# GLA score products of at most 32 rows, two low levels to a bank, and the decay of k to its tile's end on ScalarE alone

## The chip, the cores and the metric

The kernel runs on one core of a Trainium2 chip. Its time is the device time of one launch in microseconds (us). Before the change three runs took 2829.29, 2830.95 and 2833.31 us, so the median is 2830.95. One more execution was recorded by the hardware profiler.

The engines are called as in the profile: PE is TensorE (matrix products; PEld its weight loads), DVE is VectorE, ACT is ScalarE, POOL is GpSimd, SP is SyncE, which issues most DMAs. Each engine has one queue of instructions and takes them in order. PE writes only to PSUM, eight banks of 512 fp32 numbers on each of 128 partitions.

## The reference: what is computed

A streaming encoder of two layers, one with a retention mixer and one with gated linear attention (GLA), each followed by a convolutional feed-forward block, over 1024 frames of a new stream and 32 frames of a running one. The change touches the GLA mixer alone, whose core is, for each of 4 heads (q and k of 128, v of 256):

```python
def gla_chunk(S, xs):
    q, k, v, lg = xs
    b = jnp.cumsum(lg, axis=1)
    expo = b[:, :, None] - b[:, None, :]
    expo = jnp.where(causal[None, :, :, None, None], expo, -jnp.inf)
    A = jnp.einsum('bihd,bjhd,bijhd->bhij', q, k, jnp.exp(expo))
    intra = jnp.einsum('bhij,bjhe->bihe', A, v)
    cross = jnp.einsum('bihd,bhde->bihe', q * jnp.exp(b), S)
    bL = b[:, -1]
    S_new = jnp.exp(bL)[..., None] * S + jnp.einsum('bjhd,bjhe->bhde', k * jnp.exp(bL[:, None] - b), v)
    return S_new, intra + cross
```

The scores A weigh each pair of frames by a decay that differs by channel, exp(b_i - b_j). The factor k * exp(bL - b) carries k to the end of its tile for the state.

## The kernel before

**Units and tiles.** The 1056 frames are three spans (`CM`: 384, 384 and 288 frames). A unit is one head with one span; the 12 units go head by head. A span is cut into tiles of 128 frames (`minors`): three in the first two spans; in the third two, and one of the 32 frames of the running stream.

**Scores in levels.** Within a tile the pairs (j, i) are split by the block size s at which j and i part: for each s in 64, 32, 16, 8, 4, 2, 1, j lies in the first half of a block of 2s and i in the second. `weigh` makes for each level a tensor X[s] in which the first halves hold k times exp(b at the middle minus b) and the second halves q times exp(b minus b at the middle); one product of the two is the score. GpSimd subtracts (L968, L972), ScalarE takes the exponential (`expln`, L1189), VectorE multiplies (L970, L974). `weigh` also makes kd, which is k times exp(bL - b): GpSimd subtracts b at the tile's end (L988, three times a unit), ScalarE takes the exponential over the span, VectorE multiplies by k (L992), and ScalarE makes eL, exp(bL), tile by tile.

**The score products** (`scores`) are in fp32 and go into two PSUM banks, `lv0` and `lv1`, that `small()` hands out in turn. The first bank is zeroed by a product with a tile of zeros (L1001), and then gets for each tile the products of 32 frames with themselves (L1005) and the levels 64, 32 and 16 (L1010: products of 64, 32 and 16 rows). VectorE multiplies it by a mask into A (L1015). Each of the levels 8, 4, 2 and 1 has a bank of its own with products of 32 rows and 16 columns (L1023), from which VectorE copies the wanted elements into A under a mask (L1028). Then kd is transposed into the next bank (L1036), and A and kd are split in two parts of less precision each (L1044 to L1048, `stack_left` at L253 and L255).

**The rest of a unit.** `project` makes q, k and the gate of the next unit (L127 to L129, L936) in a pair of banks `pj`. `mix` makes v (`value`, L240 to L248), and per tile the state and the output (`attend`, L1117 to L1143). The last `attend` of a unit, its norm (`finish`, L1157 to L1164, which scales oraw) and its `store` come within the next unit: `store` transposes the output oraw in two halves (L1170) into the next two banks of `small()`, from which ScalarE copies (L1172) and a DMA stores.

**What sets the order.** The program is written in the order project (next unit), finish (last unit), scores, store (last unit), mix, weigh (next unit). When the kernel is built, a scheduler orders each engine's instructions by its own estimates and by the tiles' buffers: so value products stand between the score products, and the norm's small operations between the masks. At run time each engine keeps that order and waits by semaphores.

## Time and profile before

| | |
|---|---|
| median of 3 runs | 2830.95 us (2829.29 to 2833.31) |
| profiled execution | 2831.14 us, its span 2829.4 us, granted TensorE clock 0.997 |
| busy share of the span | PE 98%, PEld 94%, DVE 74%, ACT 47%, POOL 10% |
| GLA stage | about 1623 to 1943 us of the span: 320 us, the 12 units |
| in the GLA stage | PE busy 310 us, DVE 239, ACT 181, POOL 93 |

In the profile, a line number is that of the kernel before. A group row gives line, engine, operation, tiles as out<-in without buffer numbers, the shape and the count; then busy time and the mean time of one in ns; then the idle time of the engine ahead of it and what ended it. A timeline row gives the start and the length in us; for a group of several (x8) from the first start to the last end. A product's length holds its way through the array, so that products overlap: what one costs is read from start to start. Every fp32 score product has two records.

### The profile page before, as it was taken

To read this page: it belongs to the slowest core of one execution; us is meant where nothing else is said; L and a number is where in the kernel's file an instruction comes from. 1 tells how busy PE (TensorE), PEld (TensorE's weight loads), DVE (VectorE), ACT (ScalarE), POOL (GpSimd) and SP (SyncE) were. 2 spreads that over 40 slices of the span, in tenths; PEclk is the share of its full clock that TensorE was granted. 3 is DMA by queue.
4 is the path that set the end of the run, shared out by engine and by line. 5 is a ranking of instruction groups with operands and counts; after the bars stand their busy time and mean duration, and the time that the engine had idled before them with its cause. 6 is when DMAs were issued, how large, how long until landed. Compare 5 with 4: busy or idle time off the path is not lost.

```text
span 2829.4 us, 54448 instructions
## 1 busy us (share of the span) xinstructions
PE 2763.6 (98%) x21926; PEld 2654.8 (94%) x21926; DVE 2099.9 (74%) x3497; ACT 1318.5 (47%) x2384; POOL 285.6 (10%) x517
## 2 busy tenths in 40 slices
PE   8999999999999999999999999999999999999998
PEld 8999978888899999999999989989999999999997
DVE  7777777777587878887874687874378778878756
ACT  8433344444455544444543555553244444445434
POOL 1000000000001111111000133320020111110001
PEclk9999999999999999999999999999999999999999
DMA  6333386664866222432867401114522233428673
GB/s 222 108 123 106 110 281 205 212 201 153 273 196 203 66 86 99 149 117 87 285 204 234 159 30 52 52 45 156 187 87 74 81 109 122 145 76 278 204 236 113
DMA packets 232477, 419.47 MB, mean 148 GB/s; under 512 B 27392, under 2 KB 145792, under 8 KB 231200
## 3 DMA queue, kind: packets, MB, share of 16 engines
q1 hardware_dynamic: 231680, 415.40, 44.7%
q8 instruction: 171, 2.80, 0.4%
q14 instruction: 82, 0.67, 0.1%
q10 hardware_dynamic: 544, 0.59, 0.1%
HBM read 292.08 MB, written 123.85 MB: 147 GB/s over the span
## 4 chain that ended last, share of the span: by engine, by line
PE 82%; DVE 8%; DMA 5%; ACT 3%; issue 1%; POOL 1%; SPq 0%; DVEq 0%; ACTq 0%; POOLq 0%
PE pu L341 16%; PE pu L336 16%; PE pu L340 16%; PE pd L1316 3%; PE pd L1317 3%; PE pd L1318 3%; PE psv L242 2%; PE psv L241 2%; PE psv L240 2%; PE pj L127 1%; PE pj L128 1%; PE pj L129 1%; PE pg L127 1%; PE pg L128 1%; PE pg L129 1%
## 5 line engine op out<-in xcount | busy, mean ns | idle before, releaser
L106 DVE TENSOR_TENSOR wlo<-raw,whi 128x1024 fp32r<-128x1024 f32 (+1 forms) x147 | 180.7, 1235 | 91.8 <-ACT whi L106 38.0
L1572 ACT COPY AR<-pu 128x264 f32<-128x264 f32 x264 | 99.0, 375 | 293.9 <-PE pu L341 291.2
L341 PE MATMUL pu<-XA,wgl 128*128 128x264 f32 x752 | 213.6, 284 | 0.0
L336 PE MATMUL pu<-XA,wgh 128*128 128x264 f32 x752 | 213.0, 283 | 0.0
L340 PE MATMUL pu<-XA,wgh 128*128 128x264 f32 x752 | 213.0, 283 | 0.0
L106 ACT CAST whi<-raw 128x1024 fp32r<-128x1024 f32 (+1 forms) x147 | 152.6, 1041 | 109.9 <-DMA raw<-w_ro 37.5
L1316 PE MATMUL pd<-XB,whi 128*128 128x264 f32 x552 | 158.5, 287 | 1.7 <-DVE rm L212 1.7
L1594 DVE SCALAR_TENSOR_TENSOR AR<-AR,cw 128x1058 f32<-128x1058 f32 x88 | 116.0, 1318 | 58.1 <-ACT AR L1593 55.7
L1318 PE MATMUL pd<-XB,wlo 128*128 128x264 f32 x552 | 157.5, 285 | 0.0
L1317 PE MATMUL pd<-XB,whi 128*128 128x264 f32 x552 | 157.4, 285 | 0.0
L336 PE MATMUL pu<-XA,wsh 128*128 128x264 f32 x520 | 148.3, 285 | 1.7 <-ACT AR L1572 0.9
L341 PE MATMUL pu<-XA,wsl 128*128 128x264 f32 x520 | 147.9, 284 | 0.8 <-DVE wsl L309 0.8
L309 DVE TENSOR_TENSOR wtl<-rv,wth 128x1024 fp32r<-128x1024 f32 x58 | 71.5, 1234 | 102.0 <-ACT wth L309 96.3
L340 PE MATMUL pu<-XA,wsh 128*128 128x264 f32 x520 | 147.3, 283 | 0.0
L1568 DVE TENSOR_TENSOR AR<-AR,pu 128x264 f32<-128x264 f32 (+2 forms) x440 | 144.9, 369 | 0.0
L336 PEld LDWEIGHTS pu<-XA,wgh 128*128 128x128 f32 x752 | 141.3, 188 | 0.0
L341 PEld LDWEIGHTS pu<-XA,wgl 128*128 128x128 f32 x752 | 141.2, 188 | 0.0
L340 PEld LDWEIGHTS pu<-XA,wgh 128*128 128x128 f32 x752 | 141.2, 188 | 0.0
L336 PE MATMUL pu<-XA,whi 128*128 128x264 f32 x448 | 127.3, 285 | 3.6 <-ACT XA L1463 2.3
L341 PE MATMUL pu<-XA,wlo 128*128 128x264 f32 x448 | 126.9, 285 | 1.4 <-DVE wlo L106 1.4
L340 PE MATMUL pu<-XA,whi 128*128 128x264 f32 x448 | 126.7, 284 | 0.2
L336 PE MATMUL pu<-XA,wth 128*128 128x264 f32 x408 | 116.1, 285 | 0.7 <-ACT wth L309 0.7
(497 smaller groups left out, 10464.7 us busy)
## 6 DMA issues: line engine op xcount, KB each, us to landing
raw<-w_ro SPq DMA_DIRECT2D x52, 512.0 KB, 4.9
rg<-w_up SPq DMA_DIRECT2D x44, 512.0 KB, 3.6
rv<-w_up SPq DMA_DIRECT2D x44, 512.0 KB, 3.5
scr_h<-AR SPq DMA_DIRECT2D x44, 512.0 KB, 2.7
AR<-scr_x SPq DMA_DIRECT2D x32, 528.0 KB, 5.0
scr_x<-AR SPq DMA_DIRECT2D x32, 528.0 KB, 3.9
raw<-scr_w SPq DMA_DIRECT2D x32, 512.0 KB, 4.7
AR<-scr_h SPq DMA_DIRECT2D x28, 528.0 KB, 5.1
```

The source lines that it names most:

```text
L106: last_w[:] = S.copy(hi[:, k], raw[:, k]), V.tensor_tensor(lo[:, k], raw[:, k], hi[:, k].bitcast(F32), op=ALU.subtract)
L127: PE.matmul(ps, hi[:, k], rh, start=kt == 0, stop=False)
L309: last_w[:] = S.copy(h, src), V.tensor_tensor(l_, src, h.bitcast(F32), op=ALU.subtract)
L336: mm = PE.matmul(ps, wh[:, k], x[:, 0, kt], start=m in (1, 2, 4, 5) and kt == 0, stop=False, skip_group_check=True)
L340: PE.matmul(ps, wh[:, k], x[:, 1, kt], start=False, stop=False, skip_group_check=True)
L341: mm = PE.matmul(ps, wl[:, k], x[:, 0, kt], start=False, stop=kt == 3, skip_group_check=True)
L1316: PE.matmul(o, w[0][:, k], h[0][:, :n], start=i == 0, stop=False)
L1317: PE.matmul(o, w[0][:, k], h[1][:, :n], start=False, stop=False)
L1318: self.last_mm = PE.matmul(o, w[1][:, k], h[0][:, :n], start=False, stop=i == nk - 1)
L1568: V.tensor_tensor(u[:, d:d + n], t[:, o:o + n], b[:, o:o + n], op=op)
L1572: S.copy(t, b)
L1594: V.scalar_tensor_tensor(cj, uj[:, 1:T + 3], cw[:, nt, 1:2], cj, op0=ALU.mult, op1=ALU.add)
```

## The change

The score products become no wider than 32 rows. Where the first bank was zeroed, the product of 32 frames with themselves now takes in all columns to its left as well (128, 96, 64 and 32 columns for the four parts of a tile, the last part first), so that every element of the bank is written that the mask multiplication reads; level 64 becomes two products of 32 rows. The tiles come last to first. Levels 8 and 4 share a bank, and levels 2 and 1 another. The multiplication by the mask and the masked copies take all 128 rows and all three tiles in every unit. The transposes of kd, and the first half of `store`, go to the banks `pj`; the second half of `store` goes to a score bank. The tail after the last unit keeps the banks that it is given.

kd no longer uses GpSimd: a small VectorE operation makes kb = bL / TAU for the span's tiles, and ScalarE makes exp(kb - b / TAU) in one activation a tile, with kb as the bias column. eL is one activation for all tiles of one length.

```diff
@@ -893,7 +893,7 @@
         es = ExitStack()
         g1 = es.enter_context(pool("g1"))
         pp = es.enter_context(pool("gps", space=PSUM))
-        banks = [pp.tile([P, 3, P], F32, tag=f"lv{j}", name=f"lv{j}") for j in range(2)]
+        banks = [pp.tile([P, 3 * P], F32, tag=f"lv{j}", name=f"lv{j}") for j in range(2)]
         for t in banks:
             V.memset(t, 0.0)
 
@@ -984,11 +984,13 @@
 
             eL = g2.tile([P, 3], F32, tag="eL", name=f"eL{uid()}", bufs=2)
             kd = t384(g1, "kd", bufs=1)
+            kb = g2.tile([P, 3], F32, tag="kb", name=f"kb{uid()}", bufs=2)
+            for m0, m1, L in groups_of(c):
+                bL = b[:, m0 * P:m0 * P + (m1 - m0) * L].rearrange("p (m i) -> p m i", i=L)[:, :, L - 1:]
+                V.tensor_scalar(kb[:, m0:m1].unsqueeze(2), bL, 1.0 / TAU, None, op0=ALU.mult)
+                expln(eL[:, m0:m1].unsqueeze(2), bL, AF.Exp, scale=1.0 / TAU)
             for mi, (o, t0, L) in enumerate(minors(c)):
-                G.tensor_tensor(kd[:, o:o + L], b[:, o:o + L],
-                                b[:, o + L - 1:o + L].to_broadcast([P, L]), op=ALU.subtract)
-                expln(eL[:, mi:mi + 1], b[:, o + L - 1:o + L], AF.Exp, scale=1.0 / TAU)
-            expln(kd[:, :n], kd[:, :n], AF.Exp, scale=-1.0 / TAU)
+                expln(kd[:, o:o + L], b[:, o:o + L], AF.Exp, scale=-1.0 / TAU, bias=kb[:, mi:mi + 1])
             V.tensor_tensor(kd[:, :n], kd[:, :n], k[:, :n], op=ALU.mult)
             return q, k, X, qh, ql, kd, eL
 
@@ -997,41 +999,39 @@
             mins = minors(c)
             groups = groups_of(c)
 
-            pa = small()
-            PE.matmul(pa.rearrange("p m i -> p (m i)"), zero[:, :P], zero[:, P:], start=True, stop=True)
-            for mi, (o, t0, L) in enumerate(mins):
-                for a in range(0, L, TS):
-                    e = slice(o + a, o + a + TS)
-                    PE.matmul(pa[a:a + TS, mi, a:a + TS], k[:, e], q[:, e], start=True, stop=True)
+            pa = small().rearrange("p (m i) -> p m i", i=P)
+            for mi, (o, t0, L) in reversed(list(enumerate(mins))):
+                for a in range(L - TS, -1, -TS):
+                    PE.matmul(pa[a:a + TS, mi, :a + TS], k[:, o + a:o + a + TS], q[:, o:o + a + TS],
+                              start=True, stop=True)
                 for s in (64, 32, 16):
-                    for a in range(0, L, 2 * s):
-                        if a + 2 * s > L:
-                            continue
-                        PE.matmul(pa[a:a + s, mi, a + s:a + 2 * s], X[s][0][:, o + a:o + a + s],
-                                  X[s][1][:, o + a + s:o + a + 2 * s], start=True, stop=True)
+                    m = min(s, TS)
+                    for a in [a for b in range(0, L - 2 * s + 1, 2 * s) for a in range(b, b + s, m)]:
+                        e = slice(a // (2 * s) * 2 * s + s, a // (2 * s) * 2 * s + 2 * s)
+                        PE.matmul(pa[a:a + m, mi, e], X[s][0][:, o + a:o + a + m],
+                                  X[s][1][:, o + e.start:o + e.stop], start=True, stop=True)
             A = t384(g1, "A", bufs=1)
             Av = A.rearrange("p (m i) -> p m i", i=P)
-            for m0, m1, L in groups:
-                V.tensor_tensor(Av[:L, m0:m1, :L], pa[:L, m0:m1, :L],
-                                dmask[:L, :L].unsqueeze(1).to_broadcast([L, m1 - m0, L]), op=ALU.mult)
-            for li, s in enumerate(LOW):
-
-                pl = small()
-                for mi, (o, t0, L) in enumerate(mins):
-                    for a in range(0, L, TS):
-                        e = slice(o + a, o + a + TS)
-                        PE.matmul(pl[a:a + TS, mi, a // 2:a // 2 + 16], X[s][0][:, e],
-                                  X[s][1][:, e].rearrange("p (b t) -> p b t", t=2 * s)[:, :, s:],
-                                  start=True, stop=True)
-                for m0, m1, L in groups:
-                    M, B = m1 - m0, L // (2 * s)
+            V.tensor_tensor(Av, pa, dmask.unsqueeze(1).to_broadcast([P, 3, P]), op=ALU.mult)
+            for l0 in (0, 2):
+                pl = small().rearrange("p (l m i) -> p l m i", l=2, m=3)
+                for li in (1, 0):
+                    s = LOW[l0 + li]
+                    for mi, (o, t0, L) in reversed(list(enumerate(mins))):
+                        for a in range(0, L, TS):
+                            e = slice(o + a, o + a + TS)
+                            PE.matmul(pl[a:a + TS, li, mi, a // 2:a // 2 + 16], X[s][0][:, e],
+                                      X[s][1][:, e].rearrange("p (b t) -> p b t", t=2 * s)[:, :, s:],
+                                      start=True, stop=True)
+                for li in range(2):
+                    s = LOW[l0 + li]
                     mask[0] = V.copy_predicated(
-                        Av[:L, m0:m1, :L].rearrange("p m (b t) -> p m b t", t=2 * s)[:, :, :, s:],
-                        lmask[:L, li, :L // 2].rearrange("p (b t) -> p b t", t=s).unsqueeze(1).to_broadcast(
-                            [L, M, B, s]),
-                        pl[:L, m0:m1, :L // 2].rearrange("p m (b t) -> p m b t", t=s))
-
-            pkt = small()
+                        Av.rearrange("p m (b t) -> p m b t", t=2 * s)[:, :, :, s:],
+                        lmask[:, l0 + li].rearrange("p (b t) -> p b t", t=s).unsqueeze(1).to_broadcast(
+                            [P, 3, P // (2 * s), s]),
+                        pl[:, li].rearrange("p m (b t) -> p m b t", t=s))
+
+            pkt = t384(pp, "pj", w=512)[:, :3 * P].rearrange("p (m i) -> p m i", m=3)
             for mi, (o, t0, L) in enumerate(mins):
                 PE.transpose(pkt[:L, mi], kd[:, o:o + L], ident)
             Ahv, Alv, khv, klv = [t384(g2, t, F32R, 2).rearrange("p (m i) -> p m i", i=P)
@@ -1165,21 +1165,20 @@
 
             def store(lv, room):
                 for e in range(2):
-                    pt = lv("pt")[:, :3 * P].rearrange("p (m i) -> p m i", m=3)
+                    pt = (lv("pt") if lv else small() if e else t384(pp, "pj", w=512))[:, :3 * P].rearrange("p (m i) -> p m i", m=3)
                     for mi, (o, t0, L) in enumerate(mins):
                         PE.transpose(pt[:, mi, :L], oraw[:L, mi, e * P:e * P + P], ident[:L, :L])
                     ot = room()
-                    S.copy(ot[:, :n], pt.rearrange("p m i -> p (m i)")[:, :n])
+                    w = n if lv or e == 0 else 3 * P
+                    S.copy(ot[:, :w], pt.rearrange("p m i -> p (m i)")[:, :w])
                     nc.sync.dma_start(scr_o[1][2 * h + e, :, c0:c0 + n], ot[:, :n])
             return finish, store
 
         asb = g1.tile([96, T], F32R, tag="asb", name="asb")
-        zero = g1.tile([32, P + 384], F32R, tag="zero", name="zero")
-        G.memset(zero.bitcast(F32), 0.0)
         p00 = qk_products(0, 0)
 
         def lv(name):
-            return small().rearrange("p m t -> p (m t)")
+            return small()
 
         run_tails(lv)
         table = S.preload_act_table_set("natural_log_exp_and_others")
@@ -1222,7 +1221,7 @@
                 store[0]()
             sc = scores(*u, w)
             if store:
-                store[1](lv, lambda: t384(g2, "ot"))
+                store[1](None, lambda: t384(g2, "ot"))
             h, c = u
             if c == 1 and h + 1 < GH:
                 for j in range(2):
```

What the change does to the order on the engines is shown at three places of one unit, head 2 with the second span. lv is a score bank, q, k and x the operands, kd the decayed k, pv a bank of values, oraw the output of the unit before.

TensorE, start of the unit's scores. Before:

```order
L1141 MATMUL ou_20650<-gSl_20641,qh_20162 128x256
L1001 MATMUL lv_17602<-zero 128x384
L1005 MATMUL lv_17602<-q_20237,k_20239 32x32 x4
L1010 MATMUL lv_17602<-x_1555_20512 64x64
L1010 MATMUL lv_17602<-x_1557_20519 32x32 x2
L1010 MATMUL lv_17602<-x_1559_20526 16x16 x4
```

and now:

```order
L1141 MATMUL ou_20659<-gSl_20650,qh_20169 128x256
L1005 MATMUL lv_17603<-q_20243,k_20245 32x128
L1005 MATMUL lv_17603<-q_20243,k_20245 32x96
L1005 MATMUL lv_17603<-q_20243,k_20245 32x64
L1005 MATMUL lv_17603<-q_20243,k_20245 32x32
L1011 MATMUL lv_17603<-x_1575_20522 32x64 x2
L1011 MATMUL lv_17603<-x_1577_20529 32x32 x2
L1011 MATMUL lv_17603<-x_1579_20536 16x16 x4
```

The zeroing is gone and a tile has 12 products in place of 11; the two other tiles follow in the same way.

TensorE, the low levels and what stands between them, from the last products of the first bank on. Before:

```order
L1010 MATMUL lv_17602<-x_1559_20526 16x16 x4
L1023 MATMUL lv_17603<-x_1561_20533 32x16 x12
L240 MATMUL pv_20793<-whi_20380,XA 128x256
L241 MATMUL pv_20793<-wlo_20381,XA 128x256
L242 MATMUL pv_20793<-whi_20380,XA 128x256
L240 MATMUL pv_20793<-whi_20380,XA 128x256
L241 MATMUL pv_20793<-wlo_20381,XA 128x256
L1023 MATMUL lv_17602<-x_1563_20540 32x16 [waits DVE_49]
L1023 MATMUL lv_17602<-x_1563_20540 32x16 x11
L242 MATMUL pv_20793<-whi_20380,XA 128x256
L240 MATMUL pv_20793<-whi_20380,XA 128x256
L241 MATMUL pv_20793<-wlo_20381,XA 128x256
```

and now:

```order
L1011 MATMUL lv_17603<-x_1579_20536 16x16 x4
L1023 MATMUL lv_17602<-x_1583_20550 32x16 x12
L1023 MATMUL lv_17602<-x_1581_20543 32x16 x12
L1036 MATMUL pj_20767<-ident,kd_20576 128x128 [waits DVE_49]
L1036 MATMUL pj_20767<-ident,kd_20576 128x128
L1023 MATMUL lv_17603<-x_1587_20564,k_20245 32x16 [waits DVE_49]
L1023 MATMUL lv_17603<-x_1587_20564,k_20245 32x16 x11
L1023 MATMUL lv_17603<-x_1585_20557 32x16 x12
L1036 MATMUL pj_20767<-ident,kd_20576 128x128
L240 MATMUL pv_20806<-whi_20390,XA 128x256
L241 MATMUL pv_20806<-wlo_20391,XA 128x256
L242 MATMUL pv_20806<-whi_20390,XA 128x256
```

Before, the four low levels stood in four blocks with value products between them; now they stand in two, with two or three transposes of kd between them, and the second block waits for VectorE behind those. The first transpose of oraw follows two rows further on.

VectorE, from the last step ahead of the mask multiplication to the second masked copy. Before:

```order
L983 TENSOR_TENSOR ql_20969<-e_20965,qh_20968 128x288 [waits Activation_49]
L970 TENSOR_TENSOR x_1617_20919<-d_20918,k_20638 128x2x64 [waits PE_49,Pool_49]
L1015 TENSOR_TENSOR A_20702<-lv_17602,dmask 128x384 [waits PE_49]
L1160 TENSOR_TENSOR gss_20392<-gss_20392 128x3 [waits Activation_49]
L974 TENSOR_TENSOR x_1617_20919<-d_20918,q_20636 128x2x64
L1161 SCALAR_TENSOR_TENSOR gss_20392<-gss_20392 128x3 [waits DVE_49]
L1028 COPY_PREDICATED A_20702<-lmask,lv_17603 128x24x8 [waits PE_49]
L1162 SCALAR_TENSOR_TENSOR gss_20392<-gss_20392 128x3 [waits DVE_49]
L970 TENSOR_TENSOR x_1619_20926<-d_20925,k_20638 128x4x32 [waits Pool_49]
L1164 TENSOR_SCALAR oraw_20391<-oraw_20391,gss_20392 128x256 [waits DVE_49]
L1164 TENSOR_SCALAR oraw_20391<-oraw_20391,gss_20392 128x256 x2
L1028 COPY_PREDICATED A_20702<-lmask,lv_17602 128x48x4 [waits PE_49]
```

and now:

```order
L983 TENSOR_TENSOR ql_20982<-e_20978,qh_20981 128x288 [waits Activation_49]
L1015 TENSOR_TENSOR A_20713<-lv_17603,dmask 128x384 [waits PE_49]
L1160 TENSOR_TENSOR gss_20402<-gss_20402 128x3 [waits Activation_49]
L970 TENSOR_TENSOR x_1640_20932<-d_20931,k_20647 128x2x64 [waits Pool_49]
L1161 SCALAR_TENSOR_TENSOR gss_20402<-gss_20402 128x3 [waits DVE_49]
L1028 COPY_PREDICATED A_20713<-lmask,lv_17602 128x24x8 [waits PE_49]
L1162 SCALAR_TENSOR_TENSOR gss_20402<-gss_20402 128x3 [waits DVE_49]
L974 TENSOR_TENSOR x_1640_20932<-d_20931,q_20645 128x2x64
L1164 TENSOR_SCALAR oraw_20401<-oraw_20401,gss_20402 128x256 [waits DVE_49]
L1164 TENSOR_SCALAR oraw_20401<-oraw_20401,gss_20402 128x256 x2
L1028 COPY_PREDICATED A_20713<-lmask,lv_17602 128x48x4
```

The mask multiplication comes one place earlier; the norm's operations and the scaling of oraw stay between the first and the second masked copy. The multiplication's line is 1015 in both kernels.

## The prediction

> **What bounds the kernel now.** I read the page first, for the engine that sets the end, then the busy time by stage, then the timeline of the stage that the change touches, and last its waits.
>
> ```profile
> PE 2763.6 (98%) x21926; PEld 2654.8 (94%) x21926; DVE 2099.9 (74%) x3497; ACT 1318.5 (47%) x2384; POOL 285.6 (10%) x517
> PE 82%; DVE 8%; DMA 5%; ACT 3%; issue 1%; POOL 1%; SPq 0%; DVEq 0%; ACTq 0%; POOLq 0%
> ```
>
> TensorE (PE) is busy for 98% of the span and holds 82% of the chain that ended last. The change lies in the GLA stage alone; in the windows view, that stage is this row (length, then busy time and instructions of PE, PEld, DVE, ACT, POOL, then the granted clock, DMA share and GB/s):
>
> ```profile
> 1623.00:1943.00 320.00, 310.27 (x3708) 286.99 (x3707) 239.49 (x589) 180.71 (x578) 92.55 (x125) 1.00 0.15 48
> ```
>
> PE is busy for 310 of 320 us here at a clock of 1.00, DVE for 239. So what PE saves shortens the span, unless a DVE chain that PE waits for is then too late. But a busy PE may be loading, draining or changing the width of its products, which only the spacing of starts shows. The timeline of PE in unit (head 2, second span), start and duration of each merged group:
>
> ```profile
> 1815.71 0.28 PE L1141 MATMUL ou<-gSl,qh 128*128 128x256 f32 x1
> 1815.92 0.43 PE L1001 MATMUL lv<-zero 32*128 32x384 f32 x1
> 1816.29 0.27 PE L1005 MATMUL lv<-q,k 128*32 128x32 f32 x8
> 1816.48 0.52 PE L1010 MATMUL lv<-x 128*64 128x64 f32 x11
> 1816.83 0.22 PE L1005 MATMUL lv<-q,k 128*32 128x32 f32 x1
> 1816.83 0.18 PE L1010 MATMUL lv<-x 128*16 128x16 f32 x1
> 1816.85 0.22 PE L1005 MATMUL lv<-q,k 128*32 128x32 f32 x1
> 1816.86 0.18 PE L1010 MATMUL lv<-x 128*16 128x16 f32 x2
> 1817.05 0.52 PE L1010 MATMUL lv<-x 128*64 128x64 f32 x11
> 1817.61 0.52 PE L1010 MATMUL lv<-x 128*64 128x64 f32 x11
> ...
> 1819.75 0.28 PE L241 MATMUL pv<-wlo,XA 128*128 128x256 f32 x1
> 1819.96 0.38 PE L1023 MATMUL lv<-x 128*32 128x16 f32 x24
> 1820.27 0.39 PE L242 MATMUL pv<-whi,XA 128*128 128x256 f32 x1
> 1820.49 0.28 PE L240 MATMUL pv<-whi,XA 128*128 128x256 f32 x1
> 1820.62 0.28 PE L241 MATMUL pv<-wlo,XA 128*128 128x256 f32 x1
> ...
> 1822.18 0.49 PE L1036 MATMUL lv<-ident,kd 128*128 128x128 f32 x3
> 1822.43 0.36 PE L241 MATMUL pv<-wlo,XA 128*128 128x256 f32 x1
> 1823.00 0.55 PE L1170 MATMUL lv<-ident,oraw 128*128 128x128 f32 x3 [0.21 <-DVE A L1028]
> ```
>
> An fp32 product stands as two records (24 for 12 products): two passes. The zeroing product holds PE from 1815.92 to 1816.29. Each 128-frame tile of the first bank takes 0.56 (1816.48, 1817.05, 1817.61). A low level costs more than its products: from 1819.75 to 1820.49 pass 0.74, of which the two value products take 0.12 each (1820.49 to 1820.62) and the 24 records 0.20 (they last 0.38 and one of them 0.18, the same 0.18 as the 16-wide rows). The remaining 0.30 is going into the narrow products and out again. And L1170 starts 0.57 after the L241 ahead of it, where 0.12 is usual. The waits view gives these waits (PEld is the weight load ahead of each product) between 1640 and 1925 us:
>
> ```profile
> PEld lv L1170 <- ACT kh L255: 3.3, 4, 0.9
> PEld lv L1170 <- DVE kl L1048: 2.8, 7, 0.7
> PEld lv L1170 <- DVE A L1028: 1.6, 4, 0.4
> PEld lv L1023 <- DVE A L1015: 1.0, 1, 1.0
> ```
>
> **The change part by part.** Sums are for 12 units; those of the third span have two full tiles and one of 32 frames, the others three: 32 full tiles in all.
>
> Zeroing product: 12 x 0.37 = 4.4 us gone. Only the change of width on entering stays, as it stands ahead of every block.
>
> First bank: a full tile had 11 products, two of its widths (64 and 32) in turn; it gets 12, none wider than 32 rows, so each belongs to one quarter of the array. By quarter the columns are 32+64+32+16, 64+64+16, 96+32+16 and 128+16: 144 in each. The trace has no pass of 96 or 128 columns beside three others, so I bound a pass from two rows, that of L1036 at 1822.18 and its group:
>
> ```profile
> L1036 PE MATMUL lv<-ident,kd 128*128 128x128 f32 x32 | 5.5, 274 | 0.0
> ```
>
> From below: three transposes of 128 columns, one pass each, last 0.49 and one of them 0.27, so they start 0.11 apart; 144 columns in two passes would be 0.25. From above: 12 products of 16 columns in 0.20 are 0.067 for each product of a quarter, and by the column 144 would take 0.60. The two rows make a line, a pass of 16 columns 0.033 and of 128 0.11, which is 0.022 + 0.0007 per column; the quarter with four products then takes 2 x (0.044 + 0.066 + 0.044 + 0.033) = 0.38. I take that, since a product has a fixed part that the bound from above counts per column. The gain is 0.18 a tile, 32 x 0.18 = 5.8 us, with bounds of 32 x 0.31 = 9.9 and of -1.3. The small tiles I leave at nothing: they have two products as before.
>
> The trace starts L1010 and the next tile's L1005 in mixed order (1816.83 to 1816.86), so a free quarter runs ahead. The Trainium skill says otherwise (TensorE: Matmul & The Clock Gate, "Part 3: Packing small matmuls"): products start and end in strict program order; these rows do not agree.
>
> Pairs: the order shows four narrow blocks a unit before (the first bank with one level, then three levels, each between value products) and two after (the first bank with a pair, then a pair behind the transposes of kd). Two blocks less are 2 x 0.30 a unit, 24 x 0.30 = 7.2 us; the products stay the same in number.
>
> Banks: the store's transposes (L1170) waited for the masks and for kh and kl, because both halves turned in the two score banks. Now the first half and kd's transposes go into the pj banks, and the second half into the bank of the first pair. The three rows of L1170 make 7.7 us, and all of it goes.
>
> kd without GpSimd:
>
> ```profile
> L988 POOL TENSOR_TENSOR kd<-b 128x128 f32<-128x128 f32 x29 | 18.8, 673 | 3.1 <-PE lv L1036 3.1
> L1189 ACT ACTIVATE eL<-b 128x1 f32<-128x1 f32 x33 | 4.9, 192 | 0.0
> L1189 ACT ACTIVATE kd<-kd 128x384 f32<-128x384 f32 x7 | 3.6, 519 | 0.1
> L1189 ACT ACTIVATE d<-d 128x128 f32<-128x128 f32 x16 | 4.0, 302 | 1.9 <-POOL d L968 1.9
> ```
>
> GpSimd loses 36 subtractions of some 0.67; ACT gets three activations of 0.30 and one eL for one of 0.52 and three of 0.19: 1.09 in either case, beside bias columns. DVE gets one small operation of 0.17 a unit (as L1157 below), and in the third span's units five wider operations on the scores in place of ten. I count all of it as nothing: kd can be made once the unit before has transposed its own (the 3.1 us that L988 waits for L1036) and is read a unit of some 27 us (320 / 12) later. If that cover failed, the transposes of kd would wait for ACT, up to the 1.09 a unit, 13 us.
>
> New waits: with the first bank 0.37 + 3 x 0.18 earlier and less other work between, PE now comes to the second pair before the multiplication by the mask has emptied the bank that it reuses, and to L1170 before oraw is scaled. The DVE chain of this unit:
>
> ```profile
> 1816.65 0.17 DVE L1157 TENSOR_SCALAR gss<-gss 128x3 f32<-128x3 f32 x1
> 1816.97 0.46 DVE L983 TENSOR_TENSOR ql<-e,qh 128x288 fp32r<-128x288 f32 x1 [0.15 <-ACT qh L982]
> 1818.04 0.29 DVE L970 TENSOR_TENSOR x<-d,k 128x128 f32<-128x128 f32 x1 [0.61 <-PE lv L1010]
> 1818.25 0.55 DVE L1015 TENSOR_TENSOR A<-lv,dmask 128x384 f32<-128x384 f32 x1
> 1818.79 0.29 DVE L974 TENSOR_TENSOR x<-d,q 128x128 f32<-128x128 f32 x1
> 1819.07 0.36 DVE L1028 COPY_PREDICATED A<-lmask,lv 128x192 f32<-128x192 uint32 x1
> 1819.33 0.63 DVE L1162 SCALAR_TENSOR_TENSOR gss<-gss 128x3 f32<-128x3 f32 x1
> 1819.88 0.28 DVE L970 TENSOR_TENSOR x<-d,k 128x128 f32<-128x128 f32 x1
> 1820.08 0.87 DVE L1164 TENSOR_SCALAR oraw<-oraw,gss 128x256 f32<-128x256 f32 x3
> ```
>
> The mask multiplication can start at 1817.43, when L983 ends, and ends at 1817.98. PE is through the first bank at 1815.92 + 3 x 0.38 = 1817.06, through the pair of 24 products at 1817.46, through two kd transposes at 1817.9 (0.2 of the 0.30 is for coming out, an estimate): a wait of about 0.1. The second pair (0.4), coming out (0.2), a transpose (0.11) and four value products (0.48) end at 1819.27. The first oraw is scaled 1.83 + 0.29 (a third of 0.87) after the multiplication started (1818.25 to 1820.08), at 1819.55, and its signal arrives about 0.1 later: a wait of 0.4. So 0.5 a unit; bounds 0.05, if L1162's 0.63 shrinks to the 0.17 of L1157 with GpSimd's kd work gone, and 0.9, if both steps come out twice as late. Queued behind are the value products and attend; all of PE waits. 12 x 0.5 = 6.0 us, bounds 0.6 and 11.
>
> The sum: 4.4 + 5.8 + 7.2 + 7.7 - 6.0 = 19.1 us less. The profiled execution took 2831.14 us, with a span of 2829.4; the median of the three runs is 2830.95, 0.2 beside it, so the median should come out at 2812 us.
>
> **The rivals.** (1) The quarters go in program order, wave by wave: 2 x (0.11 + 0.066 + 0.044 + 0.033) = 0.51 a tile; the gain there is 1.6 in place of 5.8 and the time 2816. For it speaks that no row shows unlike widths side by side; against it the mixed starts above. The strict order that the Trainium skill states (TensorE: Matmul & The Clock Gate, Part 3) would come out like this. (2) DVE becomes the bound of the unit: the waits come to 1.2 a unit, 14 us, and the time to 2820. For it: DVE is 75% busy in the stage and stands in order between the first bank and L1170. Against it: 80 us free in 320. (3) The change doesn't save the entries and exits, because wide transposes next to the pair drain PE just as often: 7.2 less, 2819. Against it: the order has two blocks a unit. (4) No new waits and 0.25 a tile: 25 or more saved, from 2806 down to 2803 with every bound. (5) Slower: the mask multiplication comes to stand behind a weight subtraction of 1.25 on DVE,
>
> ```profile
> 1822.74 1.25 DVE L106 TENSOR_TENSOR wlo<-raw,whi 128x1024 fp32r<-128x1024 f32 x1
> ```
>
> and PE, with only kd's transposes between the pairs, waits at the second pair and at L1170 for it: from 2.1 a unit on (25 us against 25.1 gained) the kernel is slower; with two such subtractions, 2.5 a unit, 2836. Against it: the order puts both subtractions behind the last mask.
>
> **How the numbers follow.** The forecast has 0.50, rival 1 0.13, rival 2 0.12, rival 3 0.10, rival 4 0.11, rival 5 0.04. All but the last lie on one side. The range, 2804 to 2822, reaches from within rival 4 to past rivals 1 to 3; about 0.15 is left out, most of it above (rivals 2 and 3 together, rival 5). A measurement of this kernel tells 0.2% (5.7 us) from no change: faster by more than that means under 2825.3. Rivals 2 and 3 together would come out near there (0.05), and a quarter of rival 5 within the bound (0.01): 0.91 faster, 0.06 the same, 0.03 slower.
>
> **What would show it.** Right: no L1001; a full tile of the first bank every 0.38 us; two narrow blocks a unit; no wait of L1170 for kh, kl or A; a GLA stage some 19 us shorter, all stages after it alike. Waits of L1023 for A (L1015) and of L1170 for oraw (L1164) of about 0.5 a unit. Wrong: tiles of 0.5 or more (rival 1), L1170 behind oraw by over a microsecond (rival 2), 0.3 beside every transpose (rival 3).

## The result, and the profile after

The changed kernel took 2826.47 us (median of 12 runs, 2821.17 to 2830.61), the kernel before 2833.56 (12 runs beside them). The ratio is 0.9974, with a 95% interval of 0.9966 to 0.9982: faster, by some 7 us where 19 were forecast, and outside the range of 2804 to 2822. The profiled execution took 2822.85 us, with a span of 2820.7.

The page of the changed kernel, busy time and the chain, and below them the GLA stage in the windows view (length, busy time and instructions of PE, PEld, DVE, ACT, POOL, then the clock, the DMA share and GB/s):

```profile
PE 2748.1 (97%) x21978; PEld 2649.3 (94%) x21978; DVE 2099.6 (74%) x3493; ACT 1322.2 (47%) x2388; POOL 273.1 (10%) x480
PE 80%; DVE 9%; DMA 5%; ACT 4%; issue 2%; POOL 1%; SPq 0%; DVEq 0%; ACTq 0%; POOLq 0%
...
1623.00:1943.00 320.00, 303.74 (x3822) 289.67 (x3820) 244.66 (x592) 189.07 (x585) 73.08 (x89) 0.99 0.18 57
```

PE's share of the chain fell from 82 to 80%, DVE, ACT and issue rose by one each, and the stage's clock is 0.99. By the timeline, the stage lasted 301.0 us before, from its first score product (1624.8) to the first product of the phase behind it (1925.8), and lasts 291.3 after (1624.5 to 1915.7): 9.7 less. (The window of 320 us reaches into the next phase, so a unit took some 25 us before, and not 27.) The timeline of PE, again in unit (head 2, second span):

```profile
1810.20 0.28 PE L1141 MATMUL ou<-gSl,qh 128*128 128x256 f32 x1
1810.41 0.31 PE L1005 MATMUL lv<-q,k 128*32 128x128 f32 x6
...
1810.71 0.28 PE L1005 MATMUL lv<-q,k 128*32 128x128 f32 x1
1810.72 0.18 PE L1011 MATMUL lv<-x 128*16 128x16 f32 x1
...
1811.01 0.28 PE L1005 MATMUL lv<-q,k 128*32 128x128 f32 x1
...
1811.30 0.20 PE L1023 MATMUL lv<-x 128*32 128x16 f32 x2
...
1811.92 0.44 PE L1036 MATMUL pj<-ident,kd 128*128 128x128 f32 x2
1812.44 0.38 PE L1023 MATMUL lv<-x,k 128*32 128x16 f32 x24
```

There is no zeroing product, two narrow blocks are left, and a full tile takes 0.30 (1810.41, 1810.71, 1811.01, 1811.30), where 0.38 was forecast. The next tile's first products of 128 columns start beside the last ones of the tile before. So the change does in this unit what was forecast, and more. The waits of PE's weight loads in the same stretch as before, 1640 to 1925 us:

```profile
PEld lv L1023 <- DVE A L1015: 4.9, 11, 1.1
PEld ouu L1119 <- ACT vh L1102: 4.0, 3, 1.4
PEld pj L1170 <- DVE oraw L1164: 3.1, 6, 0.6
...
PEld ou L1135 <- ACT oraw L1143: 2.6, 3, 0.9
```

The waits of L1170 for kh, kl and A are gone. The first and third rows are the two new waits of the forecast. The second and fourth were in no step of it: three times each, and all six in units of the third span.

**Where they sit.** From the start of a unit's first score product to the next unit's, the unit (head 1, second span) took 26.21 us and takes 24.43, the first span after it 24.03 and 22.61. The third span's units took 24.57, 24.59 and 24.59 for heads 0, 1 and 2 and take 26.03, 24.49 and 25.92. In the last of them, PE stands still twice (timeline of PE, changed kernel):

```profile
1846.37 0.28 PE L246 MATMUL pv<-whi,xs 128*128 128x256 f32 x1
1847.84 0.36 PE L1119 MATMUL ouu<-vh,kh 128*128 128x256 f32 x1 [1.19 <-DVE gS L1124]
...
1849.20 0.58 PE L1135 MATMUL ou<-vh,Ah 128*128 128x256 f32 x1 [0.67 <-ACT oraw L1143]
1849.58 0.41 PE L1136 MATMUL ou<-vh,Al 128*128 128x256 f32 x1
1849.79 0.41 PE L1137 MATMUL ou<-vl,Ah 128*128 128x256 f32 x1
```

The queues of ScalarE and VectorE tell why. First ScalarE's timeline in this unit, after, and then in the same unit of the kernel before:

```profile
1842.16 1.12 ACT L1188 ACTIVATE d<-d 128x192 f32<-128x192 f32 x4
1845.42 0.63 ACT L1188 ACTIVATE d<-d 128x192 f32<-128x192 f32 x2 [2.14 <-POOL d L968]
1846.52 0.64 ACT L1188 ACTIVATE d<-d 128x192 f32<-128x192 f32 x2 [0.47 <-POOL d L968]
1847.06 0.46 ACT L1102 ACTIVATE vh<-pv,rc 128x256 fp32r<-128x256 f32 x1
```

```profile
1853.35 0.38 ACT L1189 ACTIVATE d<-d 128x192 f32<-128x192 f32 x1 [0.54 <-POOL d L968]
1853.62 0.47 ACT L1172 COPY ot<-lv 128x384 f32<-128x384 f32 x1
1853.99 0.48 ACT L1102 ACTIVATE vh<-pv,rc 128x256 fp32r<-128x256 f32 x1
1854.35 1.01 ACT L1189 ACTIVATE d<-d 128x192 f32<-128x192 f32 x3
```

Before, the second tile's value scaling (L1102) stood among the exponentials of the next unit's levels. After, all the exponentials of levels 16 to 2 stand ahead of it. Twice they wait for GpSimd's differences, 2.14 and 0.47 us; GpSimd itself waits for one of the two buffers of d, which VectorE must have read:

```profile
1844.31 2.18 POOL L968 TENSOR_TENSOR d<-b 128x384 f32<-128x384 f32 x2 [1.69 <-DVE x L974]
```

The row of L1119 above names VectorE and not ScalarE: the product also waits for the state update L1124, which reads the first tile's product. VectorE's timeline, after:

```profile
1846.94 0.36 DVE L970 TENSOR_TENSOR x<-d,k 128x192 f32<-128x192 f32 x1
1847.22 0.47 DVE L1124 SCALAR_TENSOR_TENSOR gS<-gS,eL,ouu 128x256 f32<-128x256 f32 x1
```

L1124 ends at 1847.69, and the value scaling at 1847.52. In VectorE's queue, three multiplications of the levels (L970, L974, L970), which need the late exponentials, now stand between that of kd and L1124; before, it was one. So both queues stand behind the same late work.

**And the clock.** Behind the two stops the products start 0.21 apart in place of 0.12 (1849.58, 1849.79). The windows view of the changed kernel, cut into stretches of 3.413 us that begin and end where its granted clock changed:

```profile
1702.20:1705.62 3.42, 1.64 (x10) 1.44 (x11) 2.35 (x8) 3.21 (x10) 0.54 (x1) 1.00 0.00 0
1705.62:1709.03 3.41, 3.41 (x13) 3.41 (x12) 2.80 (x6) 3.41 (x10) 0.00 (x0) 0.50 0.31 61
...
1773.88:1777.30 3.42, 1.99 (x15) 1.59 (x13) 3.36 (x9) 2.69 (x10) 1.65 (x3) 1.00 0.01 2
...
1845.56:1848.98 3.42, 1.78 (x13) 1.37 (x11) 3.35 (x9) 2.74 (x10) 1.47 (x2) 1.00 0.00 0
1848.98:1852.39 3.41, 3.19 (x12) 3.20 (x13) 2.32 (x6) 3.41 (x9) 0.00 (x0) 0.50 0.11 12
```

In heads 0 and 2, PE was busy for 1.64 and 1.78 of 3.42 us, and the next 3.41 us ran at half clock, which costs up to 1.7 us each. In head 1, with the same waits (1.3 and 0.9 us) but 1.99 busy, the clock stayed: this is the unit with 24.49 us.

### The profile page after: what moved, and what is told of

It is laid out like the page before. It is cut to its first block, busy times and chain, and to the rows that moved or that the text cites. A ratio compares the mean times of both kernels' runs of the same rounds, so it can differ in the third digit from the quotient of the medians.

```text
span 2820.7 us, 54472 instructions
## 1 busy us (share of the span) xinstructions
PE 2748.1 (97%) x21978; PEld 2649.3 (94%) x21978; DVE 2099.6 (74%) x3493; ACT 1322.2 (47%) x2388; POOL 273.1 (10%) x480
## 4 chain that ended last, share of the span: by engine, by line
PE 80%; DVE 9%; DMA 5%; ACT 4%; issue 2%; POOL 1%; SPq 0%; DVEq 0%; ACTq 0%; POOLq 0%
PE pu L341 16%; PE pu L336 16%; PE pu L340 16%; PE pd L1316 3%; PE pd L1315 3%; PE pd L1317 3%; PE psv L242 1%; PE psv L241 1%; PE psv L240 1%; PE pj L127 1%; PE pj L128 1%; DMA raw<-w_ro 1%; PE pj L129 1%; PE pg L127 1%; PE pg L128 1%
```

## The experiments

The experiments were made with three theories. Theory A: the lost gain is ScalarE's order in the third span, with the half clock that follows. Rival B: VectorE has become the bound of the unit. Rival C: the new kd loads ScalarE and so moves its work. A second set of runs sizes the terms of the forecast one by one. Periods are worked out from the timeline, from a unit's first score product to the next unit's; the table's three are the second and third span of head 1 and the first of head 2; "nine units" is the sum from the second unit to the tenth. Each ratio is against runs of the kernel before on the same chip.

| kernel | second, third, next first span (us) | nine units | time, us | ratio (95%) |
|---|---|---|---|---|
| before | 26.21, 24.59, 24.03 | 224.5 | 2830.66 to 2833.56 | 1 |
| changed | 24.43, 24.49, 22.61 | 217.4 | 2826.47 | 0.9974 (0.9966 to 0.9982) |
| e1_order | 24.42, 22.93, 22.57 | 210.0 | 2819.04 | 0.9957 (0.9944 to 0.9971) |
| e2_dbufs | 24.36, 23.05, 22.63 | 210.8 | 2817.31 | 0.9953 (0.9939 to 0.9968) |
| e3_kd_gpsimd | 24.52, 24.70, 22.36 | 216.8 | 2825.69 | 0.9982 (0.9971 to 0.9994) |
| e4_kd_only | 25.88, 24.10, 23.82 | 221.8 | 2830.82 | 0.9995 (0.9984 to 1.0005) |
| e5_both | 24.38, 22.29, 24.97 | 213.7 | 2820.59 | 0.9957 (0.9943 to 0.9971) |
| e6_levels | 24.46, 23.04, 22.81 | 213.4 | 2822.09 | 0.9963 (0.9950 to 0.9976) |
| e7_rows64 | 25.32, 23.24, 23.37 | 215.6 | 2818.91 | 0.9956 (0.9942 to 0.9970) |
| e8_banks | 24.87, 23.21, 22.85 | 213.4 | 2820.63 | 0.9960 (0.9948 to 0.9972) |
| e9_mask | 24.29, 22.94, 21.71 | 207.2 | 2815.06 | 0.9945 (0.9931 to 0.9958) |
| e10_fill | 24.44, 24.50, 22.59 | 215.4 | 2820.43 | 0.9961 (0.9949 to 0.9974) |
| e11_mask_both | 24.29, 22.95, 21.72 | 207.6 | 2813.47 | 0.9938 (0.9925 to 0.9950) |

**ScalarE's order** (e1): in units of the third span the exponentials of level 4 are ordered behind the second tile's value scaling, and those of levels 2 and 1 behind the copy of the first tile's output.

```diff
...
+                vh1[0] = S.activation(vh, pv, AF.Copy, scale=rc[:, m:m + 1])
+                vh1[1] = mi == 1 and c == 2
...
+        def behind(ins, s):
+            if vh1[1] and s <= 4:
+                order(ins, vh1[0] if s == 4 else ou0[0])
...
```

> The changed kernel with five ScalarE exponentials of level 4, 2 and 1 put behind other work in ScalarE's queue, in the third span's units only: level 4 behind vh of the second tile, levels 2 and 1 behind the copy of the first tile's output. Theory A (ScalarE's queue): in the changed kernel these exponentials, which wait for GpSimd, stand ahead of vh and of the output's copy, so that PE waits 1.35 us at the second tile's state product and 0.93 at its output product in each of three units, and after two of them the clock halves for 3.4 us. Then both waits fall under 0.3 us, the units of the third span with a successor take 22 to 22.5 us in place of 24.5 to 26.0, the GLA stage is 7 to 10 us shorter than in the changed kernel and no half clock is left in the stage: about 2818 us, ratio to before 0.994. Rival B (VectorE is the bound of these units): PE waits as long at another place, at most 2 us are won.

**More buffers for d** (e2): no order is set, and GpSimd gets four buffers in place of two.

```diff
-                d = t384(g1, "d")
+                d = t384(g1, "d", bufs=4)
```

> The changed kernel with four buffers in place of two for d, so that GpSimd need not wait until VectorE has used the last but one. ScalarE's queue keeps the exponentials of levels 4, 2 and 1 ahead of vh of the second tile. Theory A: they no longer wait for GpSimd, which runs ahead, so the waits of 1.35 and 0.93 us in the third span's units fall under 0.4 though the order is as before; stage 6 to 10 us shorter than in the changed kernel. Rival B (VectorE is the bound): the waits stay, within 2 us of the changed kernel; GpSimd's operations beside VectorE's could even make them longer.

**kd by GpSimd again** (e3), all else as changed; and **kd alone** changed in the kernel before (e4). The diff of both is that of `weigh` in the change, taken back and made alone.

> The changed kernel with the decay of k made as before by GpSimd; the score products, banks and masks as changed. Theory A: the order on ScalarE is the same in the third span's units, and GpSimd is later still, so PE waits there as long or longer (1.3 to 2.5 and 0.9 us); time 0 to 6 us above the changed kernel. Rival C (taking kd off GpSimd made the waits): they go, 7 us below the changed kernel.

> The kernel before with the decay of k alone changed: kb by VectorE, one activation a tile with a bias column, GpSimd without kd. As predicted it costs and gives nothing on PE: within 3 us of before. Rival C: 5 to 8 us slower than before, from waits at the products of attend.

Measured: e1 and e2 reduce the stops by different means, and both give some 7 us of the nine units back (217.4 to 210.0 and 210.8). The third span's units fall from 26.03, 24.49 and 25.92 to 22.76, 22.93 and 23.33 in e1 and 23.04, 23.05 and 23.05 in e2, and neither trace shows a half clock in the nine. By the times alone they are some 5 and 6 us faster than the changed kernel, with intervals that still overlap its own, so that the traces have to show it. PE's waits in e2, 1640 to 1925 us:

```profile
PEld lv L1023 <- DVE A L1015: 5.1, 10, 1.2
PEld pj L1170 <- DVE oraw L1164: 3.0, 6, 0.6
...
PEld ouu L1119 <- issue: 1.9, 3, 0.6
...
PEld ou L1135 <- ACT oraw L1143: 0.7, 3, 0.2
```

Neither run is as clean as was expected. In e1 the wait for vh is gone, but 2.3 us for the copy L1143 are left, and its third span's units missed the 22 to 22.5 us. In e2, L1119 still stops for up to 0.6, now for VectorE's L1124. e1 also moved VectorE's queue: L1124 stands ahead of the late multiplications there. So the two runs show that work behind GpSimd's differences, put ahead of what PE needs, made the loss; they don't divide it between the two queues.

With kd back on GpSimd the waits stand as in the changed kernel:

```profile
PEld ouu L1117 <- ACT vh L1100: 4.3, 3, 1.5
PEld ou L1133 <- ACT oraw L1141: 2.6, 3, 0.9
```

So C is out, since the waits are there without the new kd. kd alone is worth nothing that the times can tell (0.9995), although its trace has nine units that are 2.7 us shorter.

**Both remedies** (e5): e1 with four buffers of d.

> Both remedies for the third span's wait at once: ScalarE's exponentials of levels 4, 2 and 1 stand behind the second tile's value scaling (L1102 of the changed kernel) as in the first order kernel, and the differences d have four buffers. With the order alone TensorE still waited 2.3 us for the copy L1143 (three times 0.8), with the buffers alone 1.9 at L1119 and 0.7 at L1135. Theory A (ScalarE's queue stood idle for GpSimd's differences, ahead of what TensorE needs): both waits go to 0.2 or less each, the time is 0 to 2 us under the kernel with the buffers (2817.31 in its runs), so 2815 to 2817. Rival B (VectorE is the bound of the unit, and the remedies only shift which wait names it): the stage stays where either remedy left it, and waits for A and oraw take up what the others give, 2817 to 2819.

The stops in the third span are all but gone (22.29), but the next first span took 23.43, 24.97 and 25.0 us in place of 22.6, and nothing is gained over either remedy: 2820.59, where 2815 to 2817 was expected. The windows view of e5 there, second row the clock's fall:

```profile
1785.09:1788.50 3.41, 2.32 (x59) 1.84 (x59) 3.41 (x12) 1.86 (x6) 0.83 (x1) 0.99 0.04 12
1788.50:1791.91 3.41, 3.41 (x16) 3.41 (x17) 3.22 (x9) 2.55 (x7) 1.83 (x2) 0.51 0.28 89
```

PE now waits there for A (6.9 us over the stage, the longest 1.4). That looked like rival B, which the mask runs below test.

**Pairs undone** (e6): e2 with each low level in a bank of its own again.

```diff
-            for l0 in (0, 2):
+            for s in LOW:
                 pl = small().rearrange("p (l m i) -> p l m i", l=2, m=3)
-                for li in (1, 0):
-                    s = LOW[l0 + li]
...
```

> The kernel with four buffers of d, with the pairs undone: each of the levels 8, 4, 2 and 1 again in a bank of its own, products and masked copies otherwise the same. Four narrow blocks a unit in place of two. If entering and leaving a narrow block costs 0.30, as forecast, 24 more of them are 7.2 us; the second bank behind the first now comes with value products between, so up to 5 us of the waits for A (L1015) can go. Theory A: 2 to 7 us over the kernel with the buffers (2817.31), 2819 to 2824, and each block shows 0.25 to 0.35 beside its products. Rival (blocks cost nothing of their own, since wide transposes stand beside them anyhow): within 1 us of it or faster by the waits, 2812 to 2818.

A block costs in the rows of e6 what the forecast said:

```profile
1807.51 0.29 PE L240 MATMUL pv<-whi,XA 128*128 128x256 f32 x1
1807.72 0.38 PE L1021 MATMUL lv<-x 128*32 128x16 f32 x24
1808.03 0.39 PE L241 MATMUL pv<-wlo,XA 128*128 128x256 f32 x1
1808.26 0.28 PE L242 MATMUL pv<-whi,XA 128*128 128x256 f32 x1
```

From 1807.51 to 1808.26 are 0.75, less two value products (0.24) and the 24 records (0.20): 0.31. Two blocks are 0.6 a unit; but the units are only 0.0 to 0.2 longer than in e2 (24.46, 23.04, 22.81). The rest was waited away before: the wait for oraw is 1.0 us here, 3.0 in e2, and that for A 4.4 in place of 5.1. The nine units are 2.5 longer, of which up to 1.7 is a half clock in one of them. The time (2822.09) lies in the range of theory A, but the interval of its ratio overlaps that of e2.

**A product of 64 rows again** (e7): e2 with level 64 as one product.

```diff
-                    m = min(s, TS)
+                    m = s
```

> The kernel with four buffers of d, with level 64 again as one product of 64 rows in place of two of 32 (11 products a full tile, two widths in turn, all else alike). Theory A (products of 64 rows hold two quarters of the array and keep quarters from running apart): a full tile of the first bank takes 0.45 to 0.56 in place of 0.30, 32 x 0.15 to 0.26 is 5 to 8 us: 2822 to 2825. Rival (the tile's time is a price for each product, or for its columns): 0.28 to 0.32 a tile and 2816 to 2818.

```profile
1806.46 0.53 PE L1011 MATMUL lv<-x 128*64 128x64 f32 x12
...
1807.13 0.53 PE L1011 MATMUL lv<-x 128*64 128x64 f32 x12
```

A tile takes 0.67, with one product fewer: more than before the change (0.56) and more than theory A said. For the 24 full tiles of the nine units that is 8.9 us; they are 4.8 longer than in e2, as the second pair no longer waits for A (5.1 us in e2, no such row in e7). The time (2818.91) doesn't tell them apart, since both intervals are some 4 us wide to each side; the trace does.

**The banks back** (e8): e2 with kd's transposes and both halves of the store in the score banks.

```diff
-            pkt = t384(pp, "pj", w=512)[:, :3 * P].rearrange("p (m i) -> p m i", m=3)
+            pkt = small().rearrange("p (m i) -> p m i", m=3)
...
-                    pt = (lv("pt") if lv else small() if e else t384(pp, "pj", w=512))[:, :3 * P]...
+                    pt = (lv("pt") if lv else small())[:, :3 * P]...
```

> The kernel with four buffers of d, with the transposes of kd and both halves of the store in the two score banks again, as before the change. Theory A (7.7 us of waits went because the banks were freed): the waits of L1170 for kh, kl and A come back with 4 to 8 us, less what the waits for A ahead of the second pair (5 us) give, as value products stand ahead of it again: 2817 to 2823. Rival (those waits were due to GpSimd's kd, which came late and slowed VectorE): L1170 waits under 2 us for kh, kl and A, and the time is 2812 to 2817.

```profile
PEld lv L1170 <- DVE A L1028: 3.9, 9, 0.6
PEld lv L1023 <- DVE A L1015: 3.5, 10, 0.6
PEld lv L1036 <- DVE A L1028: 2.4, 6, 0.4
...
PEld lv L1170 <- ACT kh L255: 2.1, 4, 0.6
...
PEld lv L1170 <- DVE kl L1048: 0.7, 3, 0.2
```

9.1 us of the old kind of wait come back (3.9 + 2.4 + 2.1 + 0.7; those of L1170 alone are 6.7), while the wait for oraw (3.0) goes and that for A falls from 5.1 to 3.5. The nine units are 2.6 longer. Theory A holds by the trace (the intervals of the ratios overlap here too), and freeing the banks is worth about a third of the waits that it removes.

**The mask first on VectorE** (e9 on e2, e11 on e5): the split of qh and the norm from L1160 on are made after the multiplication by the mask and ordered behind it, and so is the next unit's first product with k.

```diff
...
+            first = V.tensor_tensor(Av, pa, dmask.unsqueeze(1).to_broadcast([P, 3, P]), op=ALU.mult)
+            order(split_q(), first)
+            mask[1] = first
+            if norm:
+                norm(first)
...
```

> The kernel with four buffers of d; on VectorE the multiplication by the mask (L1015 of the changed kernel) is put ahead of the split of qh (L983), the norm's small operations from L1160 on and the next unit's first product with k (L970), which stood before it and wait for ScalarE. Theory A (the waits of the second pair for A are a matter of order in VectorE's queue): they fall from 5.1 us (10 times) to under 2, the waits for oraw (3.0) rise by at most 2, a gain of 1 to 4 us: periods of 69.2 to 69.8 us a head in place of 70.05, time 2813 to 2817. Rival B (VectorE's chain from the first bank to oraw is the bound whatever its order): what the waits for A lose, those for oraw gain; periods within 0.2 of 70.05 a head, 2817 or more.

> The same order on VectorE in the kernel with both remedies for the third span. There the first span's units lost what the third span's had won: periods of 23.43 (25.0 where the clock fell to half) in place of 22.6, with a wait of 1.4 us of the second pair for A, since L1015 stood behind the split of qh and the norm, which waited for ScalarE. Theory A: that wait goes to under 0.5, no half clock falls at these places, periods are 24.4, 22.3 and 22.6, 69.3 a head, and the time is 2812 to 2816. Rival B (VectorE is the bound): 70 a head or more stay, 2817 to 2820.

The waits of e9 (its L1031 is L1023, its L1186 is L1170):

```profile
PEld lv L1031 <- DVE A L1019: 3.5, 10, 0.6
...
PEld pj L1186 <- DVE oraw L1180: 1.9, 6, 0.5
```

Both fell, A from 5.1 to 3.5 (not under 2, as theory A had it) and oraw from 3.0 to 1.9; rival B said that one would take what the other gave. The first span's units went from 22.63 to 21.71, and the nine units are 3.6 shorter; by the times alone e9 can't be told from e2. In e11 the loss of e5 is gone (21.72, no half clock in the nine), but so is what e5 had won in the third span (22.95). It is the fastest kernel measured here, 0.9938 of the kernel before, though its interval overlaps that of e9.

**Idle time filled with useless products** (e10): the changed kernel, where the value products of the 32-frame tile, which end where PE stops for L1119, get eight more ahead of them.

```diff
+                for _ in range(8 if c == 2 and mi == 2 else 0):
+                    PE.matmul(pv, xs[:, 0], wpart(0)[0], start=True, stop=True)
                 value_rows(pv, wpart, t0, xs)
```

> The changed kernel with useless work in the third span: ahead of the value products of the tile of 32 frames, the first of them is done eight more times (8 x 0.12 = 0.95 us, overwritten by the real one). They end where TensorE stood idle for L1102's vh at L1119 (1.35 over the usual spacing, then 0.92 for the copy L1143). In the changed kernel the clock went to 0.50 for 3.41 us behind that idle time in two of the three such units, where TensorE was busy for 0.48 and 0.52 of the grid stretch of 3.413 us before, and stayed at 1.00 in the one where it was busy for 0.58. Theory (a stretch of the 3.413 us grid in which TensorE is busy for less than about half is followed by one at half clock): no half clock in these units, their periods are 24.4 to 24.6 in place of 26.03 and 25.92, and the kernel is some 3 us faster for doing more work: stage 288 in place of 291.3 us, time about 2823. Rival 1 (the clock falls for another reason, such as a long wait as such): the half clock stays, and the periods too. Rival 2 (the eight products aren't hidden): 0.95 more a unit, 2.9 us slower, less what the clock gives.

```profile
1703.24:1706.66 3.42, 2.50 (x16) 2.10 (x15) 2.34 (x6) 3.20 (x8) 0.28 (x1) 1.00 0.00 0
1706.66:1710.07 3.41, 3.41 (x21) 3.41 (x20) 2.89 (x8) 2.78 (x10) 0.00 (x0) 1.00 0.52 120
```

With 2.50 us busy in place of 1.64, the clock stays at 1.00, in head 2 as well. The third span's units take 24.50, 24.50 and 24.67 in place of 26.03, 24.49 and 25.92: more work, less time. The 2.8 us that this gives are partly lost in one unit of the second span (25.10 for 24.39), whose cause stays open. The ratio is 0.9961 against 0.9974; their intervals overlap, so it is the trace that shows it. The filling also shortens the stop itself (the wait for vh from 1.4 to 0.6), so that this run alone doesn't put rival 1 out, a long wait as such. What speaks against it is the changed kernel: three units with the same waits, and a half clock behind two of them.

## Why the prediction was wrong

**Zeroing product, 4.4 us:** right; nothing in the rows takes its place.

**First bank:** right in kind, too small. 0.30 a tile and not 0.38, so 8.3 us and not 5.8. The next tile's products start beside the last ones of the tile before, so rival 1 is out; e7 shows that a single product of two quarters among them takes it all back.

**Pairs, 7.2 us, and new waits, 6.0:** the price of a block (0.31) is right, so the ground of rival 3 is out, though its result nearly came. The two new waits come to 8.0 us (4.9 + 3.1); the first is the larger, where 0.1 and 0.4 a unit were forecast. By e6 the two terms belong together: what a block less saves, PE mostly waits for instead, and the net is about 1 to 3 us.

**Banks, 7.7 us:** the waits that it names went, and e8 brings them back. But that cost and the new waits overlap too: 2.6 us in nine units, 3.5 in twelve at the same rate.

**kd as nothing:** right by the times (e4: 0.9984 to 1.0005). Nothing in PE's waits names kd.

**The step that failed** is "So 0.5 a unit ... 12 x 0.5 = 6.0 us". It walked one unit of the second span, through PE and VectorE alone, and took it for all twelve. In the third span's units the change moves ScalarE's exponentials ahead of a value scaling that PE needs, and VectorE's multiplications by them ahead of the state update. That order stood in the built program before any run, and the wait of ScalarE for GpSimd's d (1.9 us at one form of L1189) was among the rows quoted. It cost some 7 us of nine units, waits and half clock together (217.4 against e1's 210.0 and e2's 210.8). Without it, the nine units come out at 14.5 and 13.7 us less than before; nine twelfths of the forecast 19.1 are 14.3. That these agree is in part luck, since the terms above missed in both directions: the first bank gave 2.5 us more, the banks some 4 less.

**What stays open.** This step isn't the whole miss. Over the whole stage e1 and e2 are 16.7 and 16.4 us shorter than before, and their times only 12 and 13. The unit that starts the stage gains next to nothing (41.5 before, 41.4 in the changed kernel). What follows the stage takes 4.2 and 5.5 us longer in their traces than before; half-clock stretches fall there, two in e1 and one in e2 where the kernel before has none until its end, but no run shows why.

**What no step held** is the clock: a stop was counted at its own length, and behind two of the three came up to 1.7 us more. The mean granted clock of whole runs doesn't show these two: it is 0.9948 for the changed kernel, and 0.9946 and 0.9952 for e1 and e2, which have no half clock in the nine units. Such stretches fall in other phases too.

**Rival 2** (VectorE the bound, 2820) is the nearest in time, for another reason: e9 moves VectorE's order and both its waits fall. Which part of the new score products makes the scheduler put the exponentials first was not tried.

## What to carry to other kernels

When an edit lets a scheduler order the queues anew, walk one unit of every kind through every engine that feeds the bound engine, those that are mostly idle too: here ScalarE, 47% busy, and GpSimd, 10%, held up PE. A queue that stands behind a producer with two buffers could be freed here by its order or by more buffers, and the one-word edit did as well. After a stop on TensorE, look at the granted clock behind it before pricing the stop.

## What was unexpected in the hardware

The half clock comes in stretches of 3.413 us on a fixed grid: the two starts in the windows above, 1705.62 and 1848.98, are 143.36 apart, 42 x 3.413. In each of the 13 traces all half-clock stretches start on such a grid. I compared PE's records in each stretch at full clock with the clock of the next one, without the last 40 us of each kernel. With PE busy for under 0.46 of a stretch, all 36 next ones ran at half clock; between 0.46 and 0.60, 21 of 88; over 0.60, 9 of 10,348, of which six lie at about 31 us, near the kernel's start, and three soon after a unit's start, among narrow products (one of them in e5's rows above). In those last 40 us, one stretch busy for 0.43 kept its clock (e6), so these are counts and no hard limits. A stop of about 1.4 us in one stretch thus mostly costs its own length alone, and two stops in one stretch can cost more; as the grid lies elsewhere in each trace, so do the stretches that fall under the mark. The Trainium skill (TensorE: Matmul & The Clock Gate, "Part 1: The HAM clock gate") gives the window as 3413 ns and free-running, and these traces agree. Under "HAM oscillation" on the same page it puts the rule as no idle gap over some 3.4 us; here they differ, since stops of 1.19 and 0.67 us sufficed.

The other surprise is the price of one 64-row product among 32-row ones: 0.67 a tile against 0.30, with one product fewer.
